# Low parts of activation forms by a negative and an adding transfer, and the norm's parts in runs of 64, in a Griffin-style layer on one core

## The chip, the core and the metric

The kernel runs on one core of one Trainium2 chip. A core has a matrix engine (TensorE, PE in the profile), a vector engine (VectorE, DVE), an engine for activations (ScalarE, ACT), a general engine (GpSimd, POOL) and an engine that only issues transfers (SyncE, SP). Each engine works through its own list of instructions in order and waits on semaphores for the others. Operands live in SBUF (128 partitions); TensorE writes into PSUM, eight banks of 128 x 512 float32 numbers, which VectorE and ScalarE can read and GpSimd's work here does not. Transfers (DMAs) are issued by SP, ACT or POOL and run on 16 DMA engines that all of them share.

The metric is the time of one execution on the device, in microseconds (us). The kernel before has a median of 806.9 us over three runs.

## What is computed

One layer of a bidirectional trunk on x of 512 positions by 1024 features:

```
x1 = x  + RMSNorm_post_mix( W_out( sig(a_ret) * W_ret_o(Retention(h)) + sig(a_sgu) * W_sgu_o(SGU(h)) ) )
y  = x1 + RMSNorm_post_ffn( ConvGatedMLP( RMSNorm_pre_ffn(x1) ) )

def _conv_gated_mlp(h, w_up, conv_w, conv_b, w_down):      # w_up 1024 x 5632, w_down 2816 x 1024
    hid = h @ w_up
    hid = conv over 3 neighbouring positions, per feature, + conv_b
    a, b = jnp.split(hid, 2, axis=-1)
    return (jax.nn.gelu(a) * b) @ w_down
```

The change touches two places of the second line: the norm's result h2 = RMSNorm_pre_ffn(x1), as the up projection (`h @ w_up`) reads it, and gelu(a) * b, as the down product (`@ w_down`) reads it.

## The kernel before, in words

**Three passes.** TensorE multiplies numbers of reduced precision (fp32r). To keep float32 accuracy, each operand is split into a high part, which is the number rounded to fp32r, and a low part, which is the rest; a product is then the sum of hi·hi, hi·lo and lo·hi. `split(hi, lo, src)` (lines 108 to 111) makes both parts: ScalarE copies src into hi (through `copy`, line 95) and VectorE subtracts hi from src into lo (line 111). Since `split` is a helper, weights (wf, wl, dl) and activations (fl, sl) all show as lines 95 and 111 and are told apart by their names.

**The second norm (about 440 to 483 us of the span).** The 512 positions come in four tiles of 128. For each tile `norms` makes x1 and its normed rows; `turn` (lines 1002 to 1019) transposes these on TensorE (line 1009, eight 128x128 squares into two PSUM banks), and for each square ScalarE writes the scaled high part h2h (line 1011) and VectorE then writes the low part h2l from the same square and h2h (line 1014). `turns` (line 102) is the pattern of both writes: a block of 512 holds two halves of 256, positions alternate between the halves, and so neighbouring positions are written 256 elements apart, two by two. `h2_rows` (line 1028) writes the same squares once more, in one run each. Between the turns TensorE does the last of W_out (`dn_.finish`) and the first up projections (`early`), whose three passes (lines 240, 241 and 242) read h2h and h2l.

**The up projection (about 483 to 690 us).** 22 tiles of 128 features each for a and b. Sixteen of them go in eight couples (`COUPLES`), and a couple is a `Pair`: one half is done as seven smaller products by Strassen's scheme in Winograd's form (parts 1, 2 and 3, matmuls at line 773, 128x256 each), the other by plain products of 24 matmuls each (`f_block`, lines 240 to 242). A couple needs four sums of weights: T1 (line 187) and T3 (line 188) by VectorE, T2 (line 190) and T4 (line 193) by GpSimd; each is then split into parts called wf. The order in a couple is: S1 and S2 products, a plain block, the S3 product, whose PSUM bank ScalarE copies to c (line 95), a plain block, and then a product that adds to the bank that has just been copied. The weights come from memory as blocks of 128x1024 on SP's queue, four blocks ahead (`LOOK`).

After a tile comes its convolution: ScalarE at line 1068, VectorE at lines 1071 and 1075, gelu on ScalarE (line 1082), and the product gp on VectorE (line 1084).

**Forms for the down product.** The down product too goes by the seven-product scheme, for 9 pairs of tiles (`DP`), and four tiles go plainly. `down_forms(j)` (lines 1092 to 1122) makes the activation side of pair j: four sums or differences on VectorE (lines 1105 to 1108), of which fs holds two, and then high and low parts fh and fl of fs, of b and of a (for j of 0 and 1 partly as halves of 128x256, in buffers of other places), and fa of the form A11. The first eight (`EAGER`) are made during the up projection: j from 0 to 4 once tiles 7, 9, 11, 13 and 17 are done, j from 5 to 7 with the last tiles; the ninth is made inside the products themselves. Their matmuls stand at line 1187, from about 690 us on.

**What sets the order.** The code is written for a framework that schedules each engine's list by its own estimate of times and by what depends on what; buffers go round in pools (66 blocks of 128x512; five each of two odder kinds), and whoever takes a buffer over waits for its last readers. So an edit in one function can move instructions of others.

Of the kernel before, what the change touches and what calls it, by code (L numbers as in the profile page):

```python
# [12 lines left out]
AF = mybir.ActivationFunctionType  # L13
ALU = mybir.AluOpType
# [21 lines left out]
EAGER = 8  # L36
# [4 lines left out]
PRE, FFNG, LNG, LNB = 0, 8, 16, 24  # L41
# [6 lines left out]
def tile_block(ctx: ExitStack, tc, xT, x, wall, par, cs, wsp, bsp, gpost, gffn, out):  # L48
    nc = tc.nc
# [10 lines left out]
    def blk(dt=F32, n="blk", shape=(P, S)):  # L60
        return sb.tile(list(shape), dt, tag="blk", bufs=NBLK, name=nm(n))
# [9 lines left out]
    def hi192(n, dt=F32R):  # L71
        pad("hi192")
        return sb.tile([P, S], dt, tag="hi192", bufs=5, name=nm(n))

    def lo64(n, dt=F32R):
        pad("lo64")
        return sb.tile([P, S], dt, tag="lo64", bufs=5, name=nm(n))

    def tmp(n="tmp", shape=(P, S)):
        return sb.tile(list(shape), F32, tag="tmp", bufs=6, name=nm(n))  # L80
# [7 lines left out]
    def ps(shape=(P, S)):  # L88
        return pp.tile(list(shape), F32, tag="ps", name=nm("ps"))
# [4 lines left out]
    def copy(o, i):  # L94
        return nc.scalar.activation(out=o, in_=i, func=AF.Copy)  # L95

    def two(t):
        return t.rearrange("p (n c) -> p n c", n=2)

    def turns(t, f=slice(0, 256)):  # L100
        return t.rearrange("p (n c) -> p c n", n=2)[:, f, :]

    def in_turn(o):
        return o.rearrange("p (c n) -> p n c", n=2)

    def as32(t):
        return t.bitcast(F32)

    def split(hi, lo, src):
        copy(hi, src)  # L110
        nc.vector.tensor_sub(lo, src, as32(hi))  # L111
# [156 lines left out]
    def col(i):  # L268
        return part[:, i : i + 1]
# [67 lines left out]
    for k in range(KD):  # L337
# [22 lines left out]
        for m in range(8):  # L360
            c = slice(m * P, (m + 1) * P)
# [36 lines left out]
    for t in range(NT):  # L398
        for n in range(2):
# [3 lines left out]
                out=xt, in_=xt, func=AF.Square, accum_out=ss[:, 4 * n + t : 4 * n + t + 1]  # L403
# [20 lines left out]
    for c in range(19, 1, -2):  # L424
        v.scalar_tensor_tensor(
            out=lc, in0=lc, scalar=1.0 / c, in1=lb, op0=ALU.add, op1=ALU.mult
        )
    v.scalar_tensor_tensor(out=lc, in0=lc, scalar=1.0, in1=la, op0=ALU.add, op1=ALU.mult)
    with behind():
        v.tensor_scalar(out=lg, in0=lgt, scalar1=0.0, scalar2=None, op0=ALU.min)  # L430
    v.scalar_tensor_tensor(
        out=lg, in0=lc, scalar=-2.0, in1=lg, op0=ALU.mult, op1=ALU.add
# [5 lines left out]
    for m in range(8):  # L438
        t = blk(n="qkraw")
# [292 lines left out]
    for n, acc in enumerate(t_group()):  # L732
# [3 lines left out]
        if n < 2:  # L736
            for k in (n + 2, n + 6):
                t = tmp("xT")
# [95 lines left out]
    for j in range(KD // 2):  # L834
        p = Pair(AF.Gelu_apprx_tanh, lambda: U_HOMES.pop()(), None, rbc)
# [61 lines left out]
    for j in range(KD // 2):  # L897
        for o, t in gated_pair(ogh, ogl, late if j == 0 else None):
            b = (lo64("r", F32) if j == 0 else hi192("r", F32) if j < 3 else blk(n="r"))
# [5 lines left out]
    for j in range(KD // 2):  # L905
        for i, (o, t) in enumerate(gated_pair(yh, yl)):
            v.tensor_mul(two(t), in_turn(o), two(t))
            nc.gpsimd.tensor_tensor(out=t, in0=t, in1=r[2 * j + i], op=ALU.add)
            h_, l_ = blk(F32R, "mh"), blk(F32R, "ml")
# [52 lines left out]
    h2h, h2l = [], []  # L962
# [33 lines left out]

    h2 = []

    def both(t):
        return t.rearrange("p (c n) -> p c n", n=2)  # L1000

    def turn(t, zs):
        c = slice(t * 64, (t + 1) * 64)
        pf = []
        for n in range(2):
            p = ps()
            for f in range(4):
                pf.append(p[:, f * P : (f + 1) * P])
                nc.tensor.transpose(pf[-1], zs[n][:, f * P : (f + 1) * P], ident)
            for k in range(4 * n, 4 * n + 4):  # L1010
                last = nc.scalar.activation(  # L1011
                    out=turns(h2h[k], c), in_=both(pf[k]), func=AF.Copy, scale=col(FFNG + k)
                )
                v.scalar_tensor_tensor(  # L1014
                    out=turns(h2l[k], c), in0=both(pf[k]), scalar=col(FFNG + k), in1=as32(turns(h2h[k], c)),
                    op0=ALU.mult, op1=ALU.subtract,
                )
        if t != 2:
            h2_rows(t, pf)
        return pf, last.ins  # L1020

    def h2_rows(t, pf):

        for k in range(KD):
            if t == 0 and k % 2 == 0:
                h2.append(halves("h2"))
            at = (k % 2) * 256 + (t % 2) * P
            nc.scalar.activation(
                out=h2[k // 2][t // 2][:, at : at + P], in_=pf[k], func=AF.Copy, scale=col(FFNG + k)
            )  # L1030
# [16 lines left out]
    for t in range(NT):  # L1047
        acc = [dn_.finish(t, 0)]
        if t > 1:
            turn(t - 2, zs[t - 2])  # L1050
        acc.append(dn_.finish(t, 1))
        zs[t] = norms(t, acc)
    early(0, 0)
    rows2, _ = turn(2, zs[2])
    for e in range(1, EARLY):
        early(e, 0)
    _, last3 = turn(3, zs[3])
    with tc.issue_after(last3):
        h2_rows(2, rows2)
# [23 lines left out]
        gp.append(blk(n="gp") if len(gp) < 2 * DP else (hi192, lo64)[len(gp) % 2]("gp", F32))  # L1083
        v.tensor_mul(gp[-1], ca, cb)  # L1084

    def two_parts(t):
        h_, l_ = blk(F32R, "fh"), blk(F32R, "fl")
        split(h_, l_, t)
        return h_, l_

    firsts = []

    def down_forms(j):

        a, b = gp[2 * j], gp[2 * j + 1]
        if j > 1:
            first = blk(F32R, "fa")
            first = first[:, T0], first[:, T1]
        else:
            if j == 0:  # L1100
                firsts.extend((hi192("fa"), lo64("fa")))
            first = [t[:, (T0, T1)[j]] for t in firsts]
        split(*first, a[:, T0])
        s_ = blk(n="fs")
        v.tensor_sub(s_[:, T0], a[:, T1], b[:, T1])
        v.tensor_sub(s_[:, T1], s_[:, T0], a[:, T0])
        v.tensor_sub(a[:, T0], a[:, T0], a[:, T1])
        v.tensor_add(a[:, T1], b[:, T0], s_[:, T1])
        sh, sl = two_parts(s_)
        forms_ = dict(zip(("A11", "S1", "S2"), (first, (sh[:, T0], sl[:, T0]), (sh[:, T1], sl[:, T1]))))  # L1110
        if j > 1:
            for (h_, l_), n in ((two_parts(b), ("A12", "A22")), (two_parts(a), ("S3", "S4"))):
                forms_.update((n, (h_[:, t], l_[:, t])) for n, t in zip(n, (T0, T1)))
        else:
            for (h_, l_), parts_ in (
                ((hi192("fh"), lo64("fl")), (("A12", b, T0), ("S4", a, T1))),
                ((blk(F32R, "fh"), blk(F32R, "fl")), (("S3", a, T0), ("A22", b, T1))),
            ):
                for (n, src, t), to in zip(parts_, (T0, T1)):
                    forms_[n] = h_[:, to], l_[:, to]  # L1120
                    split(*forms_[n], src[:, t])
        dforms.append(forms_)

    def tile_done(i, o):
        gated(*(conv(t, 2 * i + s_) for s_, t in enumerate(o)))
        if i < COUPLES[-1][1]:
            if i in (7, 9, 11, 13, 17):
                down_forms(len(dforms))
        elif len(dforms) < EAGER:
            down_forms(len(dforms))  # L1130
# [16 lines left out]
    while i < NF:  # L1147
        if i in couples:
            p = Pair(None, lambda: tmp("c"), (h2h, h2l, h2forms))
# [84 lines left out]
    for j in range(DP):  # L1234
        if j < WHOLE:
            whole.append(two_parts(gp[2 * DP + j]))
        if j == 4:
            down_forms(late.pop(0))
        products(m, j, *((steps, LOOK - 1) if j == DP - 1 else ()))
        if j in (3, 5):  # L1240
            w = w_get()
            for t in range(NT):
                add_whole(m, t, [j // 2 - 1], [w], j == 5)
            if j == 5:
                copy(c22, m[M8])
# [241 lines left out]
```

## Time and profile before

| | us |
|---|---|
| median of three runs | 806.9 |
| lowest and highest run | 806.28, 809.85 |
| profiled execution, whole | 809.66 |
| its span in the profile | 807.9 |
| TensorE busy | 791.6 |
| VectorE busy | 664.9 |
| ScalarE busy | 443.3 |
| GpSimd busy | 84.8 |

The span is the time between the first and the last recorded instruction; 1.76 us of the profiled execution lie outside it. An engine is busy while one of its instructions runs; waits, branches and the issuing of transfers are not counted. A line such as "PE ps L773 <- ACT c L95: 2.7, 3, 1.0" says that TensorE, about to write ps at line 773, waited for ScalarE's write of c at line 95, for 2.7 us in three places, at most 1.0 at once. In a group of instructions, "x18 | 12.3, 685" means 18 of them, 12.3 us together and 685 ns on the mean. In a timeline, a row starts with the start in us and the duration, and ends, in square brackets, with the idle time before it and what ended that.

### The profile page before, as it was taken

The page shows a single profiled execution, that of the slowest core. Times are in us where ns is not written, and L with a number is a line of the kernel's source. Part 1 is how long each engine was busy: PE and PEld are TensorE (multiplying, and loading weights), DVE is VectorE, ACT ScalarE, POOL GpSimd, SP SyncE. Part 2 cuts the span into 40 slices and gives each one's busy share as a digit, 9 for nine tenths or more (in the row PEclk, how much of TensorE's full clock was granted, in tenths as well). Part 3 has the DMA queues.
Part 4 walks back from the last instruction along what each step waited for, and adds up shares of the span by engine and source line. Part 5 has one row for each costly group of instructions (what it writes and reads, how often), then busy time and mean ns, then how long its engine had stood idle before and what let it go on. Part 6 is the DMA issues. An engine that isn't in the chain of part 4 may idle for free. (4 is left out here: it accounts for less than half of the span.)

```text
span 807.9 us, 13298 instructions
## 1 busy us (share of the span) xinstructions
PE 791.6 (98%) x5163; PEld 735.3 (91%) x5163; DVE 664.9 (82%) x1115; ACT 443.3 (55%) x777; POOL 84.8 (11%) x93
## 2 busy tenths in 40 slices
PE   9989999999999999999999999999999999999996
PEld 7878998998999999999998898899998898999996
DVE  6579897877898787777765669999999989987887
ACT  6455446546676444444444687556656666544442
POOL 0010000010001111132211210110110100000001
PEclk9999999999999999999999999999999999999999
DMA  7743222222233333223359111323333341233244
GB/s 271 249 149 105 72 85 59 79 87 77 105 105 105 105 105 104 80 105 105 124 164 335 54 47 61 105 105 105 105 105 105 105 157 53 79 131 105 97 165 157
DMA packets 29903, 93.24 MB, mean 115 GB/s; under 512 B 3536, under 2 KB 4688, under 8 KB 29840
## 3 DMA queue, kind: packets, MB, share of 16 engines
q1 hardware_dynamic: 27616, 86.76, 31.4%
q0 software_dynamic: 1360, 4.46, 1.6%
q10 hardware_dynamic: 864, 1.18, 0.4%
q8 instruction: 40, 0.66, 0.3%
q14 instruction: 23, 0.19, 0.1%
HBM read 88.19 MB, written 4.19 MB: 114 GB/s over the span
## 5 line engine op out<-in xcount | busy, mean ns | idle before, releaser
L95 ACT ACTIVATE wf<-raw 128x512 fp32r<-128x512 f32 x140 | 85.4, 625 | 97.9 <-PE ps L241 30.6
L111 DVE TENSOR_TENSOR wl<-raw,wh 128x1024 fp32r<-128x1024 f32 (+1 forms) x92 | 109.6, 1200 | 34.0 <-PE ps L773 19.1
L111 DVE TENSOR_TENSOR wf<-raw,wf 128x512 fp32r<-128x512 f32 x140 | 108.7, 788 | 19.9 <-ACT wf L95 18.9
L773 PE MATMUL ps<-sh,wf 128*128 128x256 f32 x640 | 120.9, 278 | 2.0 <-ACT c L95 2.0
L95 ACT ACTIVATE wh<-raw 128x1024 fp32r<-128x1024 f32 (+2 forms) x96 | 93.0, 980 | 31.0 <-DMA raw<-wall 16.0
L773 PEld LDWEIGHTS ps<-sh,wf 128*128 128x128 f32 x640 | 101.7, 188 | 3.1 <-ACT c L95 2.4
L241 PE MATMUL ps<-h2l,wh 128*128 128x512 f32 (+1 forms) x256 | 90.4, 355 | 1.8 <-DVE h2l L1014 1.8
L240 PE MATMUL ps<-h2h,wh 128*128 128x512 f32 (+1 forms) x256 | 90.3, 355 | 0.1
L242 PE MATMUL ps<-h2h,wl 128*128 128x512 f32 (+1 forms) x256 | 90.1, 353 | 0.0
L773 PE MATMUL ps<-sl,wf 128*128 128x256 f32 x320 | 89.0, 278 | 0.0
L554 PE MATMUL ps<-wh,xh 128*128 128x512 f32 x192 | 73.5, 383 | 0.0
L556 PE MATMUL ps<-wh,xl 128*128 128x512 f32 x192 | 73.5, 383 | 0.0
L555 PE MATMUL ps<-wl,xh 128*128 128x512 f32 x192 | 73.4, 382 | 0.0
L773 PEld LDWEIGHTS ps<-sl,wf 128*128 128x128 f32 x320 | 60.1, 188 | 0.4
L1187 PE MATMUL ps<-dl,fh 128*128 128x256 f32 x216 | 59.8, 277 | 0.0
L1187 PE MATMUL ps<-dh,fh 128*128 128x256 f32 x216 | 59.7, 277 | 0.0
L1187 PE MATMUL ps<-dh,fl 128*128 128x256 f32 x216 | 59.7, 277 | 0.0
L241 PEld LDWEIGHTS ps<-h2l,wh 128*128 128x128 f32 x256 | 48.5, 189 | 6.8 <-DVE h2l L1014 2.2
L773 PE MATMUL ps<-xh,wf 128*128 128x256 f32 x288 | 54.5, 279 | 0.0
L95 ACT ACTIVATE dh<-raw 128x768 fp32r<-128x768 f32 (+1 forms) x36 | 33.6, 948 | 37.1 <-DVE raw L213 17.7
L242 PEld LDWEIGHTS ps<-h2h,wl 128*128 128x128 f32 x256 | 48.5, 190 | 5.2
L240 PEld LDWEIGHTS ps<-h2h,wh 128*128 128x128 f32 x256 | 48.3, 189 | 5.2 <-ACT h2h L1011 0.4
(314 smaller groups left out, 2037.1 us busy)
## 6 DMA issues: line engine op xcount, KB each, us to landing
raw<-wall SPq DMA_DIRECT2D x144, 512.0 KB, 3.6
x<-x SPq DMA_DIRECT2D x24, 256.0 KB, 6.0
x<-x POOLq DMA_DIRECT2D x8, 256.0 KB, 2.4
xT<-xT SPq DMA_DIRECT2D x7, 256.0 KB, 5.8
xT<-xT POOLq DMA_DIRECT2D x4, 256.0 KB, 3.4
out<-zg SPq DMA_DIRECT2D x4, 256.0 KB, 2.0
raw<-wall SPq DMA_DIRECT2D x3, 256.0 KB, 4.2
out<-zs ACTq DMA_DIRECT2D x3, 256.0 KB, 2.3
```

What stands on the lines that cost most here:

```text
L95: return nc.scalar.activation(out=o, in_=i, func=AF.Copy)
L111: nc.vector.tensor_sub(lo, src, as32(hi))
L240: nc.tensor.matmul(o, ah, bh, start=start, stop=False, skip_group_check=skip)
L241: nc.tensor.matmul(o, ah, bl, start=False, stop=False, skip_group_check=skip)
L242: nc.tensor.matmul(o, al, bh, start=False, stop=stop, skip_group_check=skip)
L554: nc.tensor.matmul(acc[t], xh[k][:, c], turns(wh[:, f]), start=k == 0, stop=False)
L555: nc.tensor.matmul(acc[t], xh[k][:, c], turns(wl[:, f]), start=False, stop=False)
L556: part_end[0] = nc.tensor.matmul(acc[t], xl[k][:, c], turns(wh[:, f]), start=False, stop=k == KD - 1)
L773: self.last = nc.tensor.matmul(o, w_[:, c], a_, start=first and k == n == 0, stop=k == 3 and n == 2, skip_group_check=True,)
L1187: nc.tensor.matmul(o, a_[:, c], w_[:, f], start=j == t == i == 0, stop=j == DP - 1 and i == 2 and n not in (M2, M3, M4), skip_group_check= ...
```

## The change

Two things. In `turn`, the parts h2h and h2l are written at the same places as before, but each instruction goes through them in another order: it writes one half's 64 positions in a run and then the other half's 64 (`two(...)[:, :, c]`), and reads PSUM at a stride of two for that (`in_turn`, line 103 of the kernel before). The helper `both` goes.

In `down_forms`, for j below `EAGER`, all parts but those of A11 come from a new function, `split_added`, in the place of `split`. ScalarE copies src to hi as before; ScalarE then writes the negative of hi into lo; and GpSimd issues a transfer from src to lo that adds what it brings to what is there, so that lo becomes src - hi. VectorE has no part in it. That concerns 28 low parts: for each of the eight fs, 128x512; twelve of a and b at 128x512 (j from 2 to 7); and eight halves at 128x256 (j of 0 and 1). On ScalarE 28 instructions are added, on VectorE 28 go, and GpSimd's list gets 28 transfers, some of which stand ahead of T2 or between T2 and T4 of a couple: for j of 0 to 3 two ahead of T2. ScalarE's list in a couple changes with it: in the couples with j of 2 and 3 the copy c of the S3 product, which stood ahead of wf(T1), now stands behind wf(T2).

```diff
-    def both(t):
-        return t.rearrange("p (c n) -> p c n", n=2)
...
                 last = nc.scalar.activation(
-                    out=turns(h2h[k], c), in_=both(pf[k]), func=AF.Copy, scale=col(FFNG + k)
+                    out=two(h2h[k])[:, :, c], in_=in_turn(pf[k]), func=AF.Copy, scale=col(FFNG + k)
                 )
                 v.scalar_tensor_tensor(
-                    out=turns(h2l[k], c), in0=both(pf[k]), scalar=col(FFNG + k), in1=as32(turns(h2h[k], c)),
+                    out=two(h2l[k])[:, :, c], in0=in_turn(pf[k]), scalar=col(FFNG + k), in1=as32(two(h2h[k])[:, :, c]),
                     op0=ALU.mult, op1=ALU.subtract,
                 )
...
-    def two_parts(t):
+    def two_parts(t, split=split):
         h_, l_ = blk(F32R, "fh"), blk(F32R, "fl")
         split(h_, l_, t)
         return h_, l_
+
+    def split_added(hi, lo, src):
+        copy(hi, src)
+        nc.scalar.activation(out=lo, in_=as32(hi), func=AF.Copy, scale=-1.0)
+        nc.gpsimd.dma_start(lo, src, accum_op=ALU.add)
...
-        sh, sl = two_parts(s_)
+        apart = split_added if j < EAGER else split
+        sh, sl = two_parts(s_, apart)
...
-            for (h_, l_), n in ((two_parts(b), ("A12", "A22")), (two_parts(a), ("S3", "S4"))):
+            for (h_, l_), n in ((two_parts(b, apart), ("A12", "A22")), (two_parts(a, apart), ("S3", "S4"))):
                 forms_.update((n, (h_[:, t], l_[:, t])) for n, t in zip(n, (T0, T1)))
...
                     forms_[n] = h_[:, to], l_[:, to]
-                    split(*forms_[n], src[:, t])
+                    apart(*forms_[n], src[:, t])
```

## The prediction

> **What bounds the kernel.** I read the page first, then the waits by engine, then stretches of 20 us, and then the lines that the change touches.
>
> ```profile
> span 807.9 us, 13298 instructions
> PE 791.6 (98%) x5163; PEld 735.3 (91%) x5163; DVE 664.9 (82%) x1115; ACT 443.3 (55%) x777; POOL 84.8 (11%) x93
> PEclk9999999999999999999999999999999999999999
> ```
>
> TensorE (PE) is busy for 791.6 of 807.9 us at an undisturbed clock, so an edit on other engines can gain only where PE waits for them. Those waits are few:
>
> ```profile
> PE ps L449 <- ACT qkraw L95: 2.9, 1, 2.9
> PE ps L773 <- ACT c L95: 2.7, 3, 1.0
> PE ps L241 <- DVE h2l L1014: 1.8, 2, 1.0
> ```
>
> The first lies near 100 us and is not touched. The third lies where the second norm's parts are made (line 1014), the second in the couples of the up projection, where the activation forms are made. Stretches show where (columns: window, sum, then busy us of PE, PEld, DVE, ACT and POOL, granted clock, DMA share, GB/s):
>
> ```profile
> 460.00:480.00 20.00, 18.07 (x144) 16.85 (x143) 14.71 (x36) 15.52 (x43) 3.94 (x7) 1.00 0.14 54
> 520.00:540.00 20.00, 19.30 (x128) 17.69 (x127) 19.85 (x30) 11.29 (x19) 3.12 (x2) 1.00 0.34 114
> 560.00:580.00 20.00, 20.00 (x134) 18.70 (x133) 19.58 (x31) 12.75 (x23) 2.93 (x2) 1.00 0.27 94
> 600.00:620.00 20.00, 19.01 (x128) 17.66 (x127) 19.55 (x31) 12.95 (x23) 2.92 (x2) 1.00 0.33 106
> 620.00:640.00 20.00, 19.01 (x128) 17.67 (x127) 19.55 (x31) 12.86 (x22) 2.92 (x2) 1.00 0.32 106
> 640.00:660.00 20.00, 20.00 (x135) 18.68 (x134) 17.80 (x27) 11.53 (x19) 2.91 (x2) 1.00 0.40 131
> 680.00:700.00 20.00, 20.00 (x124) 18.42 (x123) 20.00 (x38) 11.78 (x18) 0.00 (x0) 1.00 0.16 53
> ```
>
> PE loses 1.93 us in the norm's stretch and 0.99 in each of 600 to 620 and 620 to 640, where VectorE (DVE) is nearly full; at 640 to 660, with no forms, PE loses nothing. At 680 to 700 DVE is full and PE loses nothing: relief there is worth nothing by itself.
>
> **Part 1: runs of 64 for the norm's parts.** No instruction is added, removed or reordered; 32 ScalarE (ACT) and 32 DVE instructions get another pattern: PSUM is read at a stride of two, SBUF written in runs of 64 instead of 2.
>
> ```profile
> L1011 ACT ACTIVATE h2h<-ps,part x32: 467/490/552, 449.3 to 479.0; 128x128 fp32r<-128x128 f32 x32
> L1014 DVE SCALAR_TENSOR_TENSOR h2l<-ps,part,h2h x32: 420/444/455, 449.8 to 479.5; 128x128 fp32r<-128x128 f32 x32
> L1028 ACT ACTIVATE h<-ps,part x32: 343/382/467, 456.1 to 483.0; 128x128 f32<-128x128 f32 x32
> 475.51 3.95 ACT L1011 ACTIVATE h2h<-ps,part 128x128 fp32r<-128x128 f32 x8 [0.18 <-PE ps L1009]
> L95 ACT ACTIVATE qkraw<-ps 128x512 f32<-128x512 f32 x4 | 2.0, 593 | 0.0
> L95 ACT ACTIVATE gh<-ps 128x512 fp32r<-128x512 f32 x8 | 4.3, 592 | 0.0
> ```
>
> Line 1028 reads the same PSUM tiles with the same scale and writes them in one run: 382 ns against 490. The write pattern's price is thus about 0.1 us on ACT; for DVE there is no such pair, and I take the same 0.1 of its 444. The new stride on the reads shows on qkraw, which is read from PSUM at a stride of two (line 443) and takes 593 ns, against 592 for gh, read straight: free. Eight pairs of one turn run in lockstep, 3.95/8 = 0.49 us each, so a turn shortens by at most 8 x 0.11 = 0.9 us. PE can win what it waits, 1.8 us in two waits plus small gaps in the last turn; turn by turn I take 0.4, 0.5 and 0.5, in sum **1.4** (bounds: nothing if the reads eat it, 2.7 for three turns of 0.9). Behind the first two waits stands the early up projection, which then follows PE's own work; after the last turn, the same.
>
> [...]
>
> **Part 2: the adding transfers.** For the first eight forms' sets (`EAGER`), 28 low parts leave DVE: 8 of fs, 12 of gp at 128x512, 8 of gp at 128x256. For each, ACT writes the negative of the high part, and POOL issues a transfer that adds the source to it.
>
> ```profile
> L111 DVE TENSOR_TENSOR fl<-gp,fh 128x512 fp32r<-128x512 f32 x18 | 12.3, 685 | 0.2
> L111 DVE TENSOR_TENSOR fl<-fs,fh 128x512 fp32r<-128x512 f32 x9 | 6.2, 687 | 0.0
> L111 DVE TENSOR_TENSOR fl<-gp,fh 128x256 fp32r<-128x256 f32 x8 | 4.0, 544 | 0.0
> L95 ACT ACTIVATE fh<-gp 128x512 fp32r<-128x512 f32 x18 | 11.0, 621 | 5.6 <-DVE gp L1108 5.6
> L95 ACT ACTIVATE fh<-gp 128x256 fp32r<-128x256 f32 x8 | 3.3, 413 | 1.5 <-DVE gp L1108 1.0 <-DVE gp L1084 0.5
> 441.34 0.59 POOL L986 DMA_DIRECT2D x<-x  x1 [1.81 <-DVE x L984]
> x<-x POOLq DMA_DIRECT2D x8, 256.0 KB, 2.4
> x<-x SPq DMA_DIRECT2D x24, 256.0 KB, 6.0
> ```
>
> DVE: 20 x 0.686 + 8 x 0.54 = 18.0 us less. ACT: 20 x 0.62 + 8 x 0.41 = 15.7 us more, on an engine that is busy 12 to 13 of 20 us there. POOL: 28 issues; a plain one of this size takes 0.59 us, in sum 16.5. The traffic is 24 transfers' worth of 256 KB among streams that use a third of the engines: nothing. Where it bears on the end is inside a couple, here the one with forms set 2 (start, duration, engine, line):
>
> ```profile
> 599.78 0.63 ACT L95 ACTIVATE fh<-fs 128x512 fp32r<-128x512 f32 x1 [1.95 <-DVE fs L1106]
> 600.32 0.62 ACT L95 ACTIVATE fh<-gp 128x512 fp32r<-128x512 f32 x1
> 601.66 0.63 ACT L95 ACTIVATE fh<-gp 128x512 fp32r<-128x512 f32 x1 [0.72 <-DVE gp L1108]
> 602.20 0.37 ACT L95 ACTIVATE c<-ps 128x256 f32<-128x256 f32 x1
> 605.93 0.63 ACT L95 ACTIVATE wf<-raw 128x512 fp32r<-128x512 f32 x1 [1.24 <-POOL raw L190]
> 602.75 0.69 DVE L111 TENSOR_TENSOR fl<-gp,fh 128x512 fp32r<-128x512 f32 x1
> 603.35 0.69 DVE L187 TENSOR_TENSOR raw<-raw 128x512 f32<-128x512 f32 x1
> 604.26 1.64 POOL L190 TENSOR_TENSOR raw<-raw,raw 128x512 f32<-128x512 f32 x1 [16.78 <-DVE raw L187]
> 604.29 0.27 PE L773 MATMUL ps<-h2h,wf 128*128 128x256 f32 x1
> 613.53 0.28 PE L773 MATMUL ps<-sh,wf 128*128 128x256 f32 x1
> 614.37 0.37 ACT L95 ACTIVATE c<-ps 128x256 f32<-128x256 f32 x1
> 614.80 0.39 PE L773 MATMUL ps<-sh,wf 128*128 128x256 f32 x1 [0.99 <-ACT c L95]
> ```
>
> *Gain.* PE's stall at 613.53 to 614.80 ends with a copy c that ACT reaches late because DVE is behind. In this couple three fl of 128x512 leave DVE, 3 x 0.60 = 1.8 us at the pitch of instructions that follow each other (602.75 to 603.35); in the couples of sets 0 and 1, one of 128x512 and four of 128x256. The backlog that had grown over sets 0 to 2 does not arise, and both stalls (0.99 each in the windows) go; another 0.4 us that creeps in just before them I count too. That is **2.4** (bounds 0 and 2.4). The 0.70 us at 524 (the rest of the 2.7) stays: no forms are made there.
>
> *Loss.* In the order of the changed kernel two adding transfers stand on POOL ahead of T2 (line 190), each behind its negative, and on ACT the copy c of the S3 product, which PE must see done before it adds to that bank at 604.29, has moved from 602.20 to behind wf(T2). In before's times, with ACT's pitch of 0.54 (599.78 to 600.32): fh_fs 599.78, negative 600.32 to 600.95, fh_b 600.86, its negative done at 602.02; the second issue ends at 602.61; T2 lasts 1.64, to 604.25; wf(T2) another 0.54, c 0.37: 605.16. PE would wait 0.87. But this counts DVE as late as before; with its backlog gone the forms start up to 1.5 us earlier, and the wait is nothing. Between 0 and 0.87 for sets 2 and 3 I take 0.4 each: **0.8**. In the couples of sets 0 and 1 the backlog is smaller and DVE loses five subtractions; I count nothing, with T2's and c's slack as cover.
>
> *In the tail* sets 4 to 7 move 12 low parts. DVE gets 7 us of room, ACT 7.4 more work, POOL is idle. PE waits for nothing there and the forms are used much later. Fresh waits: fh and fs of one set take over buffers whose transfers were issued one set before; at 2.4 us to land (the POOL row above) they are done by then, so nothing. If they took the 6.0 of the SP row, ACT would stall some 3 us twice, ahead of the dh copies that feed the first products; cover is its 8 idle us of 20.
>
> **Sum.** 1.4 + 2.4 - 0.8 = 3.0 us less. The profiled execution took 809.66 us (span 807.9 and 1.76 around it), so 806.7 beside it; that run is 2.8 over the median of 806.9. The same 3.0 off the median gives **803.9 us**. Half a per cent of the median, 4.03 us, is about what a measurement of this kernel can tell from no change: faster means below 802.87, slower above 810.93.
>
> **Rivals.**
> - *The full gain.* The forms start early enough that c is never late (0 instead of 0.8) and the norm's turns give 2.7: 5.1 us, 801.8. For it: DVE is the engine that sets the couple at 600 to 640. Against it: PE's two waits in the norm sum to 1.8 only.
> - *The reads eat the writes.* h2h and h2l stay near 490 and 444 ns: the norm gives nothing, 1.6 us are left, 805.3. The qkraw row speaks against it, though its instruction is four times as long.
> - *Landings are late* (6.0 us): ACT's two stalls of 3 in the tail, half of it covered, take the 3.0 back: 806.9.
> - *POOL becomes the bound; slower.* No adding transfer stands in this trace; an issue could cost less than 0.59 or, if POOL held on until it landed, 2.4 us. I took 0.59, the nearest row in size and engine. With an issue of g above 1.07, T2 starts at 600.95 + 2g and c is done 2.55 later; PE waits s = 2g - 0.79 in each of sets 2 and 3, and, as an estimate, s - 1.5 in sets 0 and 1, where no stall shows now (560 to 580). At g = 2.4 that is 2 x 4.0 + 2 x 2.5 = 13 less the gain of 3.8: 9.2 more, 816.1. The sum turns to a loss at g = 1.25 and to more than half a per cent at 1.75. For it: POOL's T2 is on the way of the copy that PE needs, with no more than 0.87 us between. Against: the issue that the trace does show takes 0.59.
>
> **How the numbers follow.** Forecast 0.36 (a gain between 1.6 and 4.5; 0.08 of it past the half per cent), full gain 0.22, reads eat the writes 0.10, late landings 0.05, POOL the bound 0.27, since its price is the one that no row shows. Faster 0.08 + 0.22 = 0.30, same 0.28 + 0.10 + 0.05 = 0.43, slower 0.27. The range reaches from 800.0, just beyond the full gain, to 813.0, an issue of some 2 us: about 0.05 lies below and 0.12 above. The forecast's own range is 802.4 to 805.3.
>
> **What the profile will show.** Right: h2h near 380 and h2l near 340 ns; PE's waits for h2l under 1 us; no fl on DVE but set 8's; DVE below 19 of 20 us at 600 to 640; the wait of line 773 for c at 613 and 634 gone; POOL's issues at line 1091 near 0.6 us. Wrong: issues above 1.2 us, or PE waiting for c right after a couple's T2 (604 and 625), or ACT waiting for an adding transfer in the tail.

## The result and the profile after

The changed kernel takes 801.75 us at the median of six runs (800.92 to 802.45), the kernel before 806.72 beside it (806.12 to 809.85): a ratio of 0.9928, with a 95% interval of 0.9909 to 0.9948. That is faster by 0.7%, past the half per cent that a measurement can tell, inside the range of 800.0 to 813.0, and 2.2 us below the forecast of 803.9, just under the forecast's own range. The profiled execution took 802.45 us.

The page's first lines and the waits of PE in the changed kernel:

```profile
span 800.7 us, 13371 instructions
PE 790.3 (99%) x5163; PEld 735.3 (92%) x5163; DVE 646.1 (81%) x1087; ACT 452.7 (57%) x805; POOL 107.7 (13%) x121
PE ps L773 <- ACT c L95: 1.3, 1, 1.3
PE ps L241 <- DVE h2l L1011: 0.5, 1, 0.5
```

PE's waits for h2l fell from 1.8 to 0.5 us and those for c from 2.7 in three places to 1.3 in one; the wait of 2.9 us for qkraw is gone, though nothing was changed there. DVE is busy for 18.8 us less, where the 28 subtractions (18.0) and the shorter h2l (3.0) would make 21.0; ACT 9.4 more: 15.5 for the negatives, 3.9 less for h2h, and 2.2 less spread over its other work. Stretches as in the prediction (the work in them lies 3 to 7 us earlier, so the wait of 520 to 540 now falls into 500 to 520):

```profile
460.00:480.00 20.00, 19.50 (x172) 19.07 (x171) 12.15 (x30) 15.24 (x48) 2.25 (x4) 1.00 0.15 54
500.00:520.00 20.00, 18.66 (x117) 16.80 (x116) 19.24 (x29) 11.44 (x22) 4.28 (x4) 1.00 0.33 109
560.00:580.00 20.00, 20.00 (x135) 18.71 (x134) 18.13 (x28) 14.18 (x27) 6.05 (x7) 1.00 0.53 138
600.00:620.00 20.00, 19.92 (x132) 18.28 (x132) 18.56 (x29) 14.57 (x27) 4.94 (x6) 1.00 0.52 143
620.00:640.00 20.00, 20.00 (x136) 18.71 (x135) 15.93 (x25) 11.61 (x20) 4.10 (x3) 1.00 0.38 117
```

Both kernels do the same 5163 matmuls in the same stages, so the start of the n-th matmul in one trace can be set against that in the other. The table gives what each stage gained (-) or lost (+) against the trace of before, in us, for all kernels of this study that are told of below. The stages end at the matmuls that before's trace has at 59.7 (the start), 484.8 (all up to the norm's end; what differs there differs after 449, but for 0.2 us in two of the kernels and 1.1 in a third, said below), 524.9 (the first couples, without forms), 636.2 (the couples with forms) and 800.4 us (the tail).

| kernel | start | norm | first couples | couples with forms | tail | from 59.7 on |
|---|---|---|---|---|---|---|
| changed | -3.27 | -2.51 | +0.78 | -2.20 | -0.02 | -3.96 |
| changed, again | -3.75 | -2.74 | +0.71 | -2.22 | -0.02 | -4.27 |
| runs of 64 alone | -3.66 | -2.51 | +0.01 | +0.05 | +0.13 | -2.31 |
| adding transfers alone | -4.38 | -0.61 | -0.09 | -2.17 | -0.02 | -2.90 |
| added for j 0 to 3 | -3.16 | -2.77 | +0.93 | -2.25 | -0.02 | -4.12 |
| added for j 4 to 7 | -3.83 | -2.14 | +0.63 | -0.05 | -0.03 | -1.59 |
| two transfers each | -4.90 | -2.44 | +0.98 | +13.75 | +0.30 | +12.60 |
| T2 of one couple on DVE | -3.00 | -1.68 | -0.82 | -1.87 | -0.02 | -4.39 |
| T2 of all couples on DVE | -3.24 | -2.97 | -0.81 | -2.82 | -0.02 | -6.62 |
| negatives, DVE adds | -3.41 | -2.42 | +0.54 | +1.37 | +4.40 | +3.88 |
| runs of 64, T2 on DVE | -3.85 | -2.70 | -0.81 | -1.78 | -0.02 | -5.32 |
| T2 and T4 on DVE | -4.90 | -2.34 | -1.09 | -2.63 | -0.02 | -6.08 |

In the norm's column, 0.2 us of the gain of the adding transfers alone and of T2 of all couples on DVE lie ahead of 449, in places that no edit touches; the kernel with T2 of one couple on DVE lost 1.1 us between 205 and 253, without a wait of PE, so that its norm won 2.8 and not 1.7. The column of the start has nothing to do with any edit: every other trace is 3 to 5 us ahead of before's there. In that one execution ACT waited for tiles of x (4.6 us in two places, against 3.0 in one in the changed kernel), PE stood still for 2.9 us, and the clock was then granted at 0.66 for a while; the changed kernel's row for the same window shows 1.00 (windows 51 to 56, before and then the changed kernel):

```profile
51.00:56.00 5.00, 5.00 (x19) 4.08 (x18) 4.47 (x9) 2.18 (x5) 0.00 (x0) 0.66 0.59 209
```

```profile
51.00:56.00 5.00, 5.00 (x25) 4.38 (x24) 2.44 (x6) 0.00 (x0) 0.00 (x0) 1.00 0.73 262
```

So the difference of the two profiled times, 7.2 us, overstates the change; from 59.7 us on it is 4.0. The medians say 5.0. The remaining 1 us was not traced to a stage; single runs of one kernel differ by more than that (before: 805.0 to 809.9 over 25 runs beside the first four experiments), mostly, as far as the profiles tell, in the start.

### The profile page after: what moved, and what is told of

It is laid out like the page before. It is cut to its first block, busy times and chain, and to the rows that moved or that the text cites. A ratio compares the mean times of both kernels' runs of the same rounds, so it can differ in the third digit from the quotient of the medians.

```text
span 800.7 us, 13371 instructions
## 1 busy us (share of the span) xinstructions
PE 790.3 (99%) x5163; PEld 735.3 (92%) x5163; DVE 646.1 (81%) x1087; ACT 452.7 (57%) x805; POOL 107.7 (13%) x121
## 4 chain that ended last, share of the span: by engine, by line
PE 89%; DVE 4%; DMA 2%; ACT 2%; POOL 1%; issue 1%; SPq 0%; POOLq 0%; DVEq 0%; ACTq 0%
PE ps L773 23%; PE ps L241 12%; PE ps L240 12%; PE ps L242 12%; PE ps L1190 11%; PE ps L554 5%; PE ps L556 5%; PE ps L555 5%; PE ps L1206 2%; DMA raw<-wall 1%; PE ps L353 1%; PE ps L854 1%; DMA x<-x 1%; ACT wh L95 1%; POOL raw L190 0%
## 5 line engine op out<-in xcount | busy, mean ns | idle before, releaser
L111 DVE TENSOR_TENSOR wl<-raw,wh 128x1024 fp32r<-128x1024 f32 (+1 forms) x92 | 106.8, 1169 | 45.0 <-PE ps L773 19.1
L1190 PE MATMUL ps<-dh,fh 128*128 128x256 f32 x216 | 59.7, 277 | 0.0
L1190 PE MATMUL ps<-dh,fl 128*128 128x256 f32 x216 | 59.7, 277 | 0.0
```

Source lines behind the costliest of these rows:

```text
L1190: nc.tensor.matmul(o, a_[:, c], w_[:, f], start=j == t == i == 0, stop=j == DP - 1 and i == 2 and n not in (M2, M3, M4), skip_group_check= ...
```

## The experiments

**Each part alone.** My theory after the first comparison was that the two parts gain in two places that have nothing to do with each other: the norm's turns and the couples with forms.

```diff
# runs of 64 alone
-        apart = split_added if j < EAGER else split
+        apart = split
# adding transfers alone: turn() as in the kernel before
-                    out=two(h2h[k])[:, :, c], in_=in_turn(pf[k]), ...
+                    out=turns(h2h[k], c), in_=both(pf[k]), ...
```

> Part 1 alone (runs of 64; every low part by VectorE as before). Theory from the two traces: the norm's turns alone give PE 2.5 us by the end of the last turn; the wait for c near 519 us grows by 0.6 us as it did in the changed kernel, since PE comes there earlier and the weights do not; the two stalls of the couples (0.99 each) stay. So 2 us less than before, ratio 0.9975, h2h near 367 and h2l near 350 ns. Rival: VectorE is full in the couples, and what the norm wins is waited away there: the ratio is 0.999 or more, with longer waits for c at 600 to 640 us.

> Part 2 alone (adding transfers; the norm's parts written two by two as before). Theory: the two stalls of 0.99 us in the couples and 0.4 us beside them go, two waits of 0.2 us for c behind T2 come, the wait of 0.70 us near 524 us stays: 2 us less than before, ratio 0.9975; h2h at 490 ns. Rival: the gain of 5 us in the medians comes mainly from this part (VectorE's 18 us work on through the tail too): 3 us less or more, ratio 0.996.

Measured: the runs of 64 alone 804.63 us, ratio 0.9978 (0.9965 to 0.9992); the adding transfers alone 803.72, ratio 0.9961 (0.9945 to 0.9976). Both are faster than before and their shares, 0.22% and 0.39%, make up the change's 0.72% within the intervals. The table shows each in its place: the first gains 2.51 us in the norm and nothing in the couples, the second 2.17 in the couples. The rival that VectorE would wait away what the norm wins is out. Three details came out otherwise. The wait near 519 us did not grow with the runs of 64 alone (+0.01). The second kernel's norm, whose code is before's, still came out 0.61 better, 0.40 of it at the first wait for h2l: so much does that stage differ between executions. And the second kernel's ratio is the rival's 0.996 and not the theory's 0.9975, though not for the reason that the rival gave: the tail won nothing (-0.02), and of the 2.9 us in its trace 2.17 are the couples' and 0.7 lie in stages whose code is before's. The norm's instructions, in the changed kernel (line, count and the shortest, median and longest ns):

```profile
L1008 ACT ACTIVATE h2h<-ps,part x32: 348/367/402, 445.9 to 473.4; 128x128 fp32r<-128x128 f32 x32
L1011 DVE SCALAR_TENSOR_TENSOR h2l<-ps,part,h2h x32: 341/350/352, 446.3 to 473.8; 128x128 fp32r<-128x128 f32 x32
470.59 3.17 ACT L1008 ACTIVATE h2h<-ps,part 128x128 fp32r<-128x128 f32 x8 [0.57 <-PE ps L1006]
```

h2h fell from 490 to 367 ns and h2l from 444 to 350, and a pair in lockstep takes 3.17/8 = 0.40 us where it took 0.49. What the prediction calls runs of 2 were runs of one: in the order of `turns` each number is written 256 elements away from the one before it. The stride of two on PSUM costs nothing: h2h (367 ns) is even a little quicker than line 1025's copy, which reads the same squares straight (380 ns). In another order, then, these writes to SBUF are quicker by 0.12 us of h2h's 0.49 and 0.09 of h2l's 0.44, and these reads of PSUM at a stride show no price.

**Which transfers count.** Adding transfers for only a part of the forms, everything else as in the changed kernel:

```diff
-        apart = split_added if j < EAGER else split
+        apart = split_added if j < 4 else split            # j of 0 to 3
+        apart = split_added if 4 <= j < EAGER else split   # j from 4 to 7
```

> The changed kernel, but adding transfers for j of 0 to 3 alone; j from 4 to 7 are split by VectorE. Theory: all that the adding transfers give lies in the couples of j 0 to 3, the tail is worth nothing: within 0.5 us of the changed kernel, ratio to before 0.993, with no stall of PE after 640 us though VectorE is fuller at 660 to 700. Rival: VectorE's relief at 660 to 700 us counts: 1 us or more slower than the changed kernel.

> The changed kernel, but adding transfers for j from 4 to 7 alone; j of 0 to 3 are split by VectorE. Theory: as with part 1 alone: ratio to before 0.9975, the stalls for c of 1 us at 600 to 640 are back. Rival: the tail counts: more than 1 us faster than part 1 alone.

Measured: 802.62 us, ratio 0.9949 (0.9931 to 0.9968), and 804.14, ratio 0.9967 (0.9952 to 0.9981). The first is 0.9 us above the changed kernel's median, not within 0.5 as expected and not the rival's 1 us either; the two ratios' intervals overlap. In the table it has all of the couples' gain (-2.25) and no loss in the tail (-0.02), although VectorE does twelve subtractions there again; the second has none of it (-0.05). Its time does not differ from the runs of 64 alone. What the change gains through adding transfers, it gains in the couples of j 0 to 3; the ones in the tail are worth nothing.

**The same kernel again, and POOL made the bound.** The changed kernel ran once more beside three others, of which the first issues every adding transfer in two pieces:

```diff
-        nc.gpsimd.dma_start(lo, src, accum_op=ALU.add)
+        nc.gpsimd.dma_start(lo[:, :128], src[:, :128], accum_op=ALU.add)
+        nc.gpsimd.dma_start(lo[:, 128:], src[:, 128:], accum_op=ALU.add)
```

> The changed kernel once more, beside the next three. Theory: what differs from run to run lies in the first 60 us and in the wait for c near 519 us, not in the parts that were changed: from 60 us on, the end of the norm's turns again 2.1 to 2.8 us earlier than before, the couples 2.2 us, the tail 0.1 or less. Rival: one of these parts differs by more than 0.5 us from the first profile.

> Each adding transfer goes as two (a quarter and three quarters of the columns): 56 issues of POOL where there were 28. Theory: an issue costs POOL 0.87 us whatever its width, so in the couples of sets 2 and 3 T2 starts 1.7 us later and PE's wait for c grows from 0.2 to 1.9 us each, in those of sets 0 and 1 from nothing to some 1 us: 3.4 to 5.4 us slower than the changed kernel, about where before was. Rival: the couples have slack now that VectorE is relieved, and POOL has 80 per cent idle: less than 1 us slower.

Measured: the changed kernel 801.71 us, ratio 0.9927 (0.99 to 0.9953), each stage behind the start within 0.3 of its first trace, the wait near 519 us again 1.3. In two pieces: 817.85 us, ratio 1.0124 (1.0097 to 1.0151), 16 us slower than the changed kernel. The issues first, in the changed kernel (line 1091) and POOL's list around T2 in the couple with j = 2:

```profile
L1091 POOL DMA_DIRECT2D fl<-fs x8: 862/874/882, 554.6 to 685.8; - x8
DMA to landing us min/median/max: 2.7/3.4/5.3
594.83 0.88 POOL L1091 DMA_DIRECT2D fl<-fs  x1 [13.98 <-ACT fl L1090]
596.02 0.86 POOL L1091 DMA_DIRECT2D fl<-gp  x1 [0.31 <-ACT fl L1090]
596.58 1.60 POOL L190 TENSOR_TENSOR raw<-raw,raw 128x512 f32<-128x512 f32 x1
```

An adding transfer takes POOL 0.87 us and lands after 3.4, against 0.59 and 2.4 for a plain one. T2 stands behind ACT's second negative and its issue, as the prediction's order had it: its record begins 0.3 us before that issue's ends, at 596.88, and T2 is done 1.3 us after it, at 598.18. Then the kernel with two pieces, POOL in the couples with j = 1 and j = 2, and PE there:

```profile
578.67 0.88 POOL L1091 DMA_DIRECT2D fl<-fs  x1 [13.62 <-ACT fh L95]
...
582.63 3.18 POOL L1092 DMA_DIRECT2D fl<-gp  x1
583.19 3.93 POOL L190 TENSOR_TENSOR raw<-raw,raw 128x512 f32<-128x512 f32 x1
...
605.62 1.92 POOL L1092 DMA_DIRECT2D fl<-gp  x1
606.19 2.92 POOL L190 TENSOR_TENSOR raw<-raw,raw 128x512 f32<-128x512 f32 x1
```

```profile
560.00:580.00 20.00, 16.74 (x101) 15.38 (x100) 16.71 (x26) 13.01 (x25) 4.91 (x7) 0.91 0.37 114
580.00:600.00 20.00, 16.96 (x112) 15.98 (x111) 13.22 (x21) 11.02 (x21) 8.41 (x9) 0.91 0.50 112
600.00:620.00 20.00, 18.12 (x120) 16.62 (x119) 16.82 (x26) 13.80 (x24) 8.18 (x8) 1.00 0.56 144
```

At j = 2 four issues stand ahead of T2 instead of two, T2 ends at 609.1, and PE loses 1.88 us in the window: the 1.9 expected. At j of 0 and 1 I was wrong by much: the scheduler put eight issues ahead of T2 there, all that the couple has, where the changed kernel has two, and PE stood for 3.3 and 3.0 us, after which its clock dropped for some 3 us: 0.91 on the mean of those windows, 0.66 in the 5 us after 570. The sum comes out: PE's waits for c went from 1.3 to 12.2 us, and three stretches of 3.4 us at half the pace (the third is shown at the end) cost, as an estimate, 5.1 more, together 16.0. So this kernel doubles the issues in two couples and quadruples those ahead of T2 in the two others; it shows that POOL has no slack in the couples, but its 16 us are no slope for one more issue.

**T2 off POOL.** The wait of 1.3 us near 519 us is the largest that the changed kernel has left. The chain behind it runs from the landing of two weight blocks through T1 to T2, which took POOL 1.83 or 1.84 us there in most traces, and 2.44 (j 4 to 7), 2.77 (j 0 to 3) and 2.77 (two transfers each) in three. Two kernels move T2 to VectorE, in that couple alone and in all couples of the up projection:

```diff
-            eng = nc.vector if i < GATE0 or i == UP0 + 2 * COUPLES[0][0] else nc.gpsimd
+            eng = nc.vector if i < GATE0 or i in (UP0 + 2 * COUPLES[0][0], UP0 + 2 * COUPLES[1][0]) else nc.gpsimd
+            eng = nc.vector if i < GATE0 or i >= UP0 else nc.gpsimd    # all of them
```

> The changed kernel with T2 of the second couple alone (line 190, near 516 us) moved from POOL to VectorE. Theory: the wait of 1.3 us for c near 519 us is set by T2 taking 1.8 to 2.8 us on POOL beside VectorE's subtractions; on VectorE it takes 0.7: the wait goes but for 0.2, about 1 us faster than the changed kernel. Rival: VectorE is 19.2 of 20 us busy there, and T2 is late on it too: within 0.3 us.

> The changed kernel with T2 of all couples of the up projection moved from POOL to VectorE. Theory: T2 no longer stands behind two adding transfers, so the waits of 0.2 us for c in sets 2 and 3 go as well, 1.4 us faster than the changed kernel. Rival: 0.7 us more for VectorE in each couple, at 18.6 of 20 us, brings back the stalls of 1 us for the later copies (608 and 629 us in the changed kernel): 1 us slower than with T2 of the second couple alone.

Measured, beside the changed kernel's 801.71: 800.74 us, ratio to before 0.9909 (0.988 to 0.9937), and 799.91, ratio 0.9907 (0.988 to 0.9933). The intervals of all three overlap; the traces tell them apart. The first couples go from +0.7 to -0.8 in both, and the couples with forms from -2.2 to -2.8 with all of them moved. There PE waits for c no more at all. ACT in the couple with j = 2:

```profile
595.10 0.61 ACT L95 ACTIVATE wf<-raw 128x512 fp32r<-128x512 f32 x1
595.61 0.36 ACT L95 ACTIVATE c<-ps 128x256 f32<-128x256 f32 x1
600.00:620.00 20.00, 20.00 (x134) 18.71 (x133) 17.95 (x31) 14.80 (x27) 3.90 (x4) 1.00 0.52 145
```

wf(T2) and the copy c come without a wait, and VectorE, which does T2 besides, is *less* busy than with T2 on POOL (17.95 of 20 us against 18.56; 641.4 against 646.1 us over the whole span). That raised the question of what had filled VectorE in the first place.

**Three kernels on VectorE's load.**

```diff
# negatives by ScalarE, the addition by VectorE
-        nc.gpsimd.dma_start(lo, src, accum_op=ALU.add)
+        nc.vector.tensor_add(lo, as32(lo), src)
# runs of 64, T2 on VectorE, no adding transfers
-            eng = nc.vector if i < GATE0 or i == UP0 + 2 * COUPLES[0][0] else nc.gpsimd
+            eng = nc.vector if i < GATE0 or i >= UP0 else nc.gpsimd
-        apart = split_added if j < EAGER else split
+        apart = split
# T2 and T4 on VectorE, with adding transfers: both lines "eng =" with i >= UP0
```

> The changed kernel with ScalarE's negatives, but VectorE adds the source to them; POOL issues nothing. VectorE has its 28 instructions back, ScalarE keeps its 28 more. Theory: the couples' gain came from VectorE's relief alone, so the stalls for c of 1 us at 600 to 640 us are back and from 60 us on it stands as part 1 alone does, 2 us slower than the changed kernel or more. Rival: the gain came from another order of the instructions: within 0.5 us of the changed kernel.

> Part 1, no adding transfers, and T2 of all couples of the up projection on VectorE. Theory: VectorE, full in the couples, gets 0.7 us more in each: 1 us or more slower than part 1 alone, PE's waits for c longer than 1 us at 560 to 640; T2 on VectorE pays only beside the adding transfers. Rival: POOL's T2 was what made VectorE's subtractions slow (1.4 to 2.2 us in the place of 0.7 to 1.2), so it pays by itself: 1 us or more faster than part 1 alone.

> The changed kernel with T2 and T4 of all couples of the up projection on VectorE; POOL issues the adding transfers and adds no weights. Theory: with T2 on VectorE, PE waits for nothing in the couples any more, so T4 has nothing to win: within 0.5 us of T2 alone on VectorE (0.991 of before). Rival: VectorE becomes full again: 1 us or more slower than that.

Measured: negatives with VectorE's addition 807.08 us, ratio 1.0001 (0.9981 to 1.0021); runs of 64 with T2 on VectorE 800.23, ratio 0.9913 (0.9888 to 0.9939); T2 and T4 on VectorE 799.94, ratio 0.9906 (0.9883 to 0.9928).

The first agrees in the sum with the theory that the couples gain by VectorE's relief: with its 28 instructions back the couples' gain is gone (+1.37 in the table), and in the medians all of what the runs of 64 win is lost again. The place was not the expected one. At 600 to 640 us, where before has its stalls, PE waited no more than 0.2 us at once; it waited 1.1 us each at 559 and 580, in the couples of sets 0 and 1, where T2 on POOL now took 2.77 us beside VectorE's additions:

```profile
556.37 2.77 POOL L190 TENSOR_TENSOR raw<-raw,raw 128x512 f32<-128x512 f32 x1 [17.25 <-DVE raw L187]
```

In the couples that is 1.3 us worse than the runs of 64 alone, with ScalarE's negatives still there; so this kernel does not tell VectorE's load from the order of the instructions. Its profiled execution was the slowest of its twelve runs (810.17, the others from 804.97 on): in the tail PE did 172 matmuls in 20 us where the other traces have 179, at a granted clock of 1.00; why stays open, and I read nothing from that column.

In the second my theory fell, and its rival held: T2 on VectorE wins by itself, 4.4 us in the medians and 3.0 in the traces from 59.7 us on against the runs of 64 alone, and no adding transfer is needed for it. VectorE in the couple with j = 2 of this kernel:

```profile
595.10 0.69 DVE L187 TENSOR_TENSOR raw<-raw 128x512 f32<-128x512 f32 x1
595.83 0.69 DVE L188 TENSOR_TENSOR raw<-raw,raw 128x512 f32<-128x512 f32 x1
596.43 0.69 DVE L190 TENSOR_TENSOR raw<-raw,raw 128x512 f32<-128x512 f32 x1
597.04 0.69 DVE L111 TENSOR_TENSOR wf<-raw,wf 128x512 fp32r<-128x512 f32 x1
597.64 0.42 DVE L812 TENSOR_TENSOR c<-ps,c 128x256 f32<-128x256 f32 x1
600.00:620.00 20.00, 19.53 (x130) 18.10 (x129) 19.83 (x33) 12.47 (x23) 1.64 (x2) 1.00 0.29 106
```

In before's trace, the subtraction beside POOL's T2 took 1.44 us and the one of 128x1024 beside T4 2.18:

```profile
605.01 1.44 DVE L111 TENSOR_TENSOR wf<-raw,wf 128x512 fp32r<-128x512 f32 x1
607.55 2.18 DVE L111 TENSOR_TENSOR wl<-raw,wh 128x1024 fp32r<-128x1024 f32 x1 [0.26 <-ACT wh L95]
```

That holds for all seven couples whose T2 stands on POOL (the first couple's is on VectorE already): in before's trace the subtraction of wf that runs beside T2 takes 1.44 to 1.76 us, the 49 others 0.67 to 0.69, and with T2 on VectorE all 56 take 0.67 to 0.69. On VectorE, T2 costs 0.69 and gives back at least 0.75 on the subtraction beside it; for VectorE it is free, and for the chain T2, wf(T2), c it is 1 us shorter. VectorE is about as full as ever (19.83 of 20; over the span 658.8 us against 661.6 with the runs of 64 alone), and PE waits only 0.5 us. Whether the shorter chain or the 2.8 us on VectorE ended the stalls, no kernel here tells apart. With T4 moved as well nothing more is won, as expected: PE had no wait left that T4 could end.

## Why the prediction was right, and where it was not

- *The range and the side.* The time lay in the range; the likeliest case, within half a per cent, did not come true. Of the prediction's cases the full gain (801.8 us) is the one that was measured (801.75), in part by luck: its two terms came as it said (2.7 and 2.4; measured 2.5 and 2.2 net), the wait near 519 us took 0.7 of it, and about 1 us of the medians' difference could not be placed.
- *The norm* was mis-sized. I took 1.4 us, held down by PE's waits of 1.8; measured were 2.5, with the change and with the runs of 64 alone. A pair became 0.10 us shorter, much as forecast (0.11). Turn by turn I had taken 0.4, 0.5 and 0.5; the matmuls' starts show 1.1 at the first wait, 0.5 at the second and 0.9 in the last turn, where PE lost small gaps that the view of waits does not list. Of the 1.1, some 0.4 may belong to before's one execution, since the adding transfers alone, with before's norm, won 0.4 there too. Less that, the change's part is about 2.1, between the 1.4 and the bound of 2.7.
- *The reads at a stride of two* are free, as the qkraw row had said (593 ns against 592): h2h takes 367 ns with them, line 1025's copy of the same squares, read straight, 380.
- *The couples' gain*, 2.4, was right: the stalls at 613 and 634 went, and with j 0 to 3 alone the gain is whole.
- *The loss by c behind T2*, 0.8, was right in kind and half as large: PE waits 0.2 us in each of sets 2 and 3 (in set 2 it resumes at 599.17 where, at the pace before, it would have at 598.96), because the forms start 1.3 us earlier against their product, as assumed.
- *The cover in sets 0 and 1* held in the changed kernel. With twice the issues it is gone, as the rival said (PE stands for 3.3 and 3.0 us there).
- *POOL's price* was 0.87 us per issue, not 0.59: under the 1.07 from which the rival's sum counted two issues in a row, and below its turning point of 1.25. The rival's mechanism is real: with four issues ahead of T2 instead of two, PE loses 1.88 us at j = 2.
- *The wait near 524 us* I had left at 0.70. It became 1.3 in the changed kernel, and stayed at 0.7 with either part alone. The traces show two ways to it: weights that land later (ACT waited 0.46 and 0.65 us for raw ahead of T1 in the changed kernel, 0.33 in sum with the runs of 64 alone, 0.56 in before), and a T2 of 2.44 or 2.77 us. All six traces of kernels with runs of 64, this T2 on POOL and some negatives lose 0.5 to 1.0 in that stage, and either part alone loses nothing; yet the kernel with j 4 to 7 loses 0.6 there with the same instructions up to there as the runs of 64 alone. Whether the change makes it likelier stays open. As a term it should have had a spread of a microsecond.
- *The tail* was worth nothing, as said; landings of 3.4 us made ACT and DVE wait 0.9 us in sum, without PE.
- *Two readings of before's trace* were wrong and bore on no term: the wait for qkraw lies at 47 to 50 us and not near 100, and the clock was not undisturbed, but at 0.66 from 51 to 56.

The step that failed is the size of the norm's term (1.4 us taken, 2.5 measured), and the wait near 524, left at 0.70, grew to 1.3; the direction and the places of the gains were right.

## What to carry to other kernels

When an engine is full and another waits for it only now and then, look at what stretches its instructions before moving its work away: here T2 on GpSimd stretched the subtraction beside it on VectorE by 0.75 us and more, where doing T2 itself takes VectorE 0.69, and in the traces moving T2 to VectorE won as much as moving 28 subtractions off it and more (3.0 us against 1.6 to 2.0, each beside the runs of 64 alone). In this kernel alternating writes to SBUF cost some 0.1 us of 0.49 and a stride of two on the reads of PSUM cost nothing (367 ns, against 380 for a straight copy of the same squares), so it pays to try the stride on the reading side. Profiles of two kernels are compared by the start of the same matmul, stage by stage; the spans alone would have given the change 3 us that belong to the first 60 us of one execution.

## What the runs showed that was not expected

An adding transfer from SBUF to SBUF holds POOL for 0.87 us whatever its width (128x128 to 128x512), half as much again as a plain one (0.59), and lands after 3.4 us (2.7 to 5.3). Issued in a row, eight of them delayed the addition behind them until 587.1, 8.4 us after the first. Where an addition on POOL and a subtraction on VectorE meet, it differs from trace to trace which of the two is stretched. Beside T4 the subtraction of 128x1024 took 2.18 us (shown above) and T4 1.28 in before's couple with j = 2, but 1.22 and 2.35 with T2 on VectorE:

```profile
598.78 1.22 DVE L111 TENSOR_TENSOR wl<-raw,wh 128x1024 fp32r<-128x1024 f32 x1
598.79 2.35 POOL L193 TENSOR_TENSOR raw<-raw,raw 128x512 f32<-128x512 f32 x1 [19.55 <-DVE wf L111]
```

So T2 on POOL, with no issue ahead of it, took 1.63 us in before's couple with j = 0 and 2.77 in the same couple with VectorE's additions (shown above), and the stage of the first couples differs by 0.6 us between two kernels with the same instructions there (runs of 64 alone and j 4 to 7). And four stalls cost PE more than their length: with two pieces per transfer, the matmuls after stalls of 3.3, 3.0 and 2.1 us followed each other at half the pace for some 3 us, as they did after the 2.9 us near 50 in before, while after the stall of 1.9 us that ended at 610.1 they did not (granted clocks of 0.66, 1.00 and 0.51 in windows behind three of these stalls, and the matmul that ended the one of 2.1):

```profile
570.00:575.00 5.00, 3.81 (x16) 3.52 (x17) 5.00 (x9) 3.81 (x8) 0.00 (x0) 0.66 0.38 147
610.00:615.00 5.00, 4.91 (x34) 4.67 (x35) 4.03 (x7) 3.55 (x7) 2.14 (x2) 1.00 0.50 93
633.00:636.00 3.00, 3.00 (x17) 3.00 (x17) 1.32 (x2) 1.48 (x3) 1.44 (x2) 0.51 0.52 79
632.39 0.38 PE L773 MATMUL ps<-h2h,wf 128*128 128x256 f32 x1 [2.10 <-ACT c L95]
```
